# GpSimd makes every fourth low half of the first mixer's weights, from the second dense product to the output projection

## The chip, the cores and the metric

One core of one Trainium2 chip runs the kernel. The metric is the device time of one execution in microseconds; the median of three executions stands for the kernel. The profile is of one further execution.

## The reference

Two blocks act on a sequence x of 256 rows and 1024 columns in fp32, one after the other. The change lies in the first one's mixer:

```python
mod = silu(c) @ w_ada + b_ada
sh1, sc1, g1, sh2, sc2, g2 = split(mod, 6)
h = rms_norm(x) * (1 + sc1) + sh1
proj = h @ w_in                        # 1024 x 3592
q_a, k_a, v_a, qk_m, v_m, o_m, gates = split(proj)
attn = head_rms_norm(moba_attention(rope(q_a), rope(k_a), v_a))
q_m, k_m = split(silu(causal_conv(qk_m)))
hm = head_rms_norm(mlstm(q_m, k_m, v_m, gates)) * sigmoid(o_m)
x = x + g1 * (concat(attn, hm) @ w_out)   # 1024 x 1024
x = x + g2 * hier_moe(rms_norm(x) * (1 + sc2) + sh2)   # 4 groups x 8 experts
```

The second block has a differential attention, a grouped-query attention with axial ropes, and two feed-forward parts.

## The kernel before

**Weights.** All weights are cut into units of 128 x 4096 fp32 (2 MB), which SyncE loads in a fixed order (`prefetch`, L304) into a ring of five slots; a slot is free again when the last reader of its unit is done. In the expert part that follows the first mixer the ring has four slots more, and SyncE is asked ahead to fill all nine.

**Split products.** An fp32 product is made of three products in the format fp32r. `split` (L511) takes a piece of 128 x 512 of a unit `w`: ScalarE rounds it to the high half `wh` (L518), VectorE subtracts it to get the low half `wl` (L520), and `mm3` (L523) issues three matmuls on TensorE: high by high (L525), then one with each low half (L526, L527). In `dense` the `wl` product is L527, in `dense_t` and `rows_into` the products run with weights as the fixed or the moving operand, so `wl` is read by L526 or L527. In the first mixer `wh` and `wl` have four buffers each, so ScalarE can make a high half only when TensorE is done with the one four before it. `behind` (L505) can tie a low half to stand behind a named instruction; it counts down and is used for a few of them.

**The first mixer.** `w_in` is multiplied unit by unit: q (before the change's place), k, v, then the gates and the mLSTM's parts; then the attention and the mLSTM, woven with those products (`weave`, L1100, the generators `mixers` and `dense_work`), and the output projection with `w_out`. Beside the products, `mixed` (L820) and `beside` interleave the products of the adaLN modulation: `ada_cols` on VectorE (L456, a product of 128 x 1024 with its sum, 32 in all) and `ada` on TensorE (L433). The rope sums of q and k are on GpSimd (L700, L703), fed by products on VectorE that read PSUM (L698 to L702); TensorE turns the result (L795). GpSimd's queue also issues the loads of small constants (`load`, L872), and scales `sub_g` (L955). In the mLSTM part VectorE makes the conv products (L1010), ScalarE its silu (L1013), VectorE the score products (L1069).

**Order.** A tile scheduler puts every engine's instructions into one order from the program and from estimated times; each engine then runs its own list in that order and waits on semaphores for what the others make. So moving instructions from one engine to another can change the order of others too. The names in the rows below are the scheduler's: `wl_1337` is one certain low half, `wh_1336` its high half, `w_868` the unit it is cut from.

Of the kernel before, what the change touches and what calls it, by code (L numbers as in the profile page):

```python
# [10 lines left out]
F32 = mybir.dt.float32  # L11
# [174 lines left out]
def block_pair_kernel(ctx: ExitStack, tc: tile.TileContext, d, out):  # L186
    nc = tc.nc
    ve, se, po, te, sy = nc.vector, nc.scalar, nc.gpsimd, nc.tensor, nc.sync
    cnt = [0]

    def mk(pool, shape, dt, tag, **kw):
        cnt[0] += 1
        return pool.tile(shape, dt, tag=tag, name=f"{tag}_{cnt[0]}", **kw)
# [29 lines left out]
    def psum_g():  # L223
        return mk(pp, [128, 512], F32, "g")
# [82 lines left out]
    def take(name):  # L307
        prefetch(pos[0] + sum(n for _, n in slots["pools"]))
        got, w = loaded[pos[0]]
        assert got == name, (got, name)  # L310
        loaded[pos[0]] = None
        pos[0] += 1
        return w
# [73 lines left out]
    def weave(*flows):  # L387

        live = [[0, n, steps] for steps, n in flows]
        while live:  # L390
            f = min(live, key=lambda f: (f[0] + 0.5) / f[1])
            f[0] += 1
            if next(f[2], live) is live:
                live.remove(f)

    def attention(n, ready, score, value, norm, turn, turn_ready=lambda: True):


        held, late = [], []

        def values():
            p, i, e = held.pop(0)
            value(p, i, e)
            if i == n - 1:
                late.append((p, norm(p)))

        for p in range(4):
            while not ready(p):
                yield
            for i in range(n):  # L410
                held.append((p, i, score(p, i)))
                if len(held) > 1:
                    values()
                if late and i >= n // 2 and turn_ready():
                    turn(*late.pop(0))
                yield
        while held:
            values()
            yield
        while not turn_ready():  # L420
            yield
        while late:
            turn(*late.pop(0))
# [49 lines left out]
    def beside(steps, vfill, nv, fill, n_p):  # L473

        done = 0
        for i, _ in enumerate(steps):
            while (done + 1) * 8 <= (i + 1) * 4 * nv:
                next(vfill)
                done += 1
            yield  # L480
        for _ in range(n_p):
            next(fill, None)
            yield
# [11 lines left out]
    def spread(m, *gs):  # L495

        for j in range(4):
            ps = psum_g()
            te.matmul(ps, ident[:, 32 * j:32 * j + 1].to_broadcast([128, 128]), m, start=True, stop=True)
            se.copy(gs[j // 2][:, j % 2 * 512:(j % 2 + 1) * 512], ps)  # L500

    parts = [None, 5]

    chain = [None, 0]
    nth_chain = itertools.count()  # L505

    def behind():

        if chain[1] == 0:
            return nullcontext()  # L510
        chain[1] -= 1  # L511
        return tc.issue_after(chain[0])

    def split(w):

        wh = mk(parts[0], [128, 512], F32R, "wh", bufs=parts[1])
        wl = mk(parts[0], [128, 512], F32R, "wl", bufs=parts[1])
        se.copy(wh, w)  # L518
        with behind():
            ve.tensor_sub(wl, w, wh.bitcast(F32))  # L520
        return wh, wl

    def mm3(ps, ah, al, bh, bl, first, last):  # L523
# [9 lines left out]
    def dense(w, hi, lo, evict):  # L533

        pss = [psum_g() for _ in range(TT)]
        for k in range(DC):
            wh, wl = split(w[:, k * 512:(k + 1) * 512])
            for t in range(TT):
                s = slice(t * 128, (t + 1) * 128)
                mm3(pss[t], hi[k][:, s], lo[k][:, s], wh, wl, k == 0, k == DC - 1)  # L540
            yield
        for t in range(TT):
            evict(t, pss[t])

    def dense_t(w, hi, lo, evict, bank):

        pss = [bank(), bank()]
        for k in range(DC):
            wh, wl = split(w[:, k * 512:(k + 1) * 512])
            for c in range(4):  # L550
                o = pss[c // 2][:, (c % 2) * T:(c % 2 + 1) * T]
                cs_ = slice(c * 128, (c + 1) * 128)
                mm3(o, wh[:, cs_], wl[:, cs_], hi[k], lo[k], k == 0 and c % 2 == 0, k == DC - 1 and c % 2 == 1)
            yield
        for i in range(2):
            evict(i, pss[i])
# [56 lines left out]
    def turn_into(hi, lo, gain, done, nh, k0=0):  # L613

        def f(p, oc):
            ps = psum()[:, :nh * T].rearrange("p (h n) -> p h n", h=nh)
            for t in range(TT):
                for h in range(nh):
                    te.transpose(ps[:, h, t * 128:(t + 1) * 128], oc[:, t, h, :], ident)
            for h in range(nh):  # L620
                scale_into(hi, lo, gain)(k0 + nh * p + h, ps[:, h, :])
            done.extend(range(k0 + nh * p, k0 + nh * (p + 1)))
        return f

    def out_proj(name, hi, lo, acc, done):

        late = []
        for u in range(2):
            w = take(name)
            for k in range(4 * u, 4 * u + 4):  # L630
                while not k in done:
                    yield
                yield from rows_into(w[:, k % 4 * D:(k % 4 + 1) * D], [k], hi, lo, acc, 0, 7, 3 * (k > 5), late)
# [186 lines left out]
    def mixed(n, steps):  # L820
        return beside(steps, vfill, MIXV[n], fill, MIXP[n])
# [49 lines left out]
    def load(v, src):  # L871
        tc.keep_in_program_order(po.dma_start(v, src))  # L872
        return v
# [4 lines left out]
    qk_g = load(mk(base, [128, 256], F32, "qk_g"), bcast(d["qk_g"], 0, 256)).rearrange("p (a n) -> p a n", a=2)  # L878
    grid = load(mk(base, [128, 256], F32, "grid"), d["const_x"][:, X_CX:X_N])

    for _ in mixed(0, range(8)):
        pass
    for n, ev in ((0, None), (1, ev_qk(kT, store_k)), (2, lambda t, ps: se.copy(va[:, t, :], ps))):
# [117 lines left out]
    def conv_work(n):  # L1001
        def ev(i, ps):
            for a in range(2):
                c = 4 * n + 2 * i + a
                u = ps[:, a * T:(a + 1) * T]
                acc = qkm[:, c, :]
                se.activation(acc, u, AF.Identity, bias=conv[:, c, 4:5], scale=conv[:, c, 3:4])
                for j in range(3):
                    z = 3 - j
                    ve.scalar_tensor_tensor(acc[:, z:], u[:, :T - z], conv[:, c, j:j + 1], acc[:, z:],  # L1010
                                            op0=OP.mult, op1=OP.add)
            if n == 1 and i == 1:
                se.activation(qkm, qkm, AF.Silu)  # L1013

        yield from dense_t(take("w_in"), hi, lo, ev, psum_g)
# [8 lines left out]
    def router_work():  # L1024

        ps = psum_g()
        for k in range(DC):
            te.matmul(ps[0:36, 0:1], wr[:, k, :], fill_col[:, k:k + 1], start=k == 0, stop=k == DC - 1)
        ve.tensor_mul(wr, wr, fill_col[:, 8:16, None].to_broadcast([128, DC, 36]))
        lT = t1([36, 128])  # L1030
        ve.tensor_add(lT, ps[0:36, 0:1].to_broadcast([36, 128]), bcol.to_broadcast([36, 128]))
        te.transpose(ps[:, 128:164], lT, ident[0:36, 0:36])
        se.copy(br, ps[:, 128:164])

    def dense_work():
        for n in range(2):
            yield from mixed(3 + n, conv_work(n))
        yield from mixed(5, dense(take("w_in"), hi, lo,
                                  lambda t, ps: se.copy(vx[:, t, :, 0:128], ps.rearrange("p (h e) -> p h e", h=4))))
        stage["vx"] = True  # L1040
        sig = mk(paa, [128, TT, 512], F32, "va")
        yield from mixed(6, dense(take("w_in"), hi, lo, lambda t, ps: se.activation(sig[:, t, :], ps, AF.Sigmoid)))
        so.append(sig)
        yield from fill
        g.extend((mk(pa, [128, D], F32, "g1"), mk(base, [128, D], F32, "g2")))
        spread(gm, *g)
        router_work()
        acc.extend([psum_g(), psum_g()] for _ in range(TT))
        yield from out_proj("w_out", oh, ol, acc, done)
# [43 lines left out]
    def mixers():  # L1093
        yield from attention(2, lambda p: True, score, value, norm,
                             turn_into(oh, ol, lambda k: og[:, k:k + 1], done, 1))
        while not stage["vx"]:
            yield
        yield from attention(2, lambda h: True, mscore, mvalue, mnorm, mturn, lambda: len(so) > 0)

    weave((mixers(), WEAVE[2][0]), (dense_work(), WEAVE[2][1]))  # L1100
    g1, g2 = g
    attn_a.close()
    ring2, ring2_close = new_pool("ring2", "right")
# [563 lines left out]
```

## Time and profile before

| what | value |
|---|---|
| median of 3 executions | 1333.07 us (1332.79 to 1334.86) |
| profiled execution | 1335.57 us |
| its span | 1333.5 us (2.07 us lie around it) |
| busy in the span: TensorE, VectorE, ScalarE, GpSimd | 1122.0 (84%), 659.8 (49%), 487.8 (37%), 145.4 (11%) us |
| GpSimd instructions counted | 194 |
| mean rate of the DMA engines | 298 GB/s |

The span is measured from the first to the last instruction on the core. The first mixer ends at about 204 us, the expert part begins there, and from 233 to 640 us it is the expert products and their weights. A busy share over the whole span says little about any one of these stretches, so the rows below are of stretches.

### The profile page before, as it was taken

The numbers are of one execution on the slowest core, as the hardware profiler recorded it, in microseconds if no ns is written. First come the engines' busy times: TensorE is split into PE (matmuls) and PEld (weight loads), VectorE is DVE, ScalarE is ACT, GpSimd is POOL, SyncE is SP. The second block draws the span as 40 slices with busy tenths as digits, with TensorE's granted clock in tenths as the row PEclk, the third lists the DMA queues.
The fourth block names the chain that finished last, engine by engine and source line by source line (L and its number), as shares of the span: only waits on it lengthen the run. The fifth ranks groups of instructions, "written<-read, shape, count | busy, mean of one in ns | idle before, by whom it ended". The sixth has DMA issues, their size and how long they took to land.

```text
span 1333.5 us, 19535 instructions
## 1 busy us (share of the span) xinstructions
PE 1122.0 (84%) x7627; PEld 814.5 (61%) x7627; DVE 659.8 (49%) x1564; ACT 487.8 (37%) x1061; POOL 145.4 (11%) x194
## 2 busy tenths in 40 slices
PE   6889997865656576666689999999999989999995
PEld 4667775431313132321267777998996766998994
DVE  4688885210202020211277777555556866555555
ACT  2445652000000000000146565554554564554552
POOL 1310000000000000000030002210114201210112
PEclk8998998988979787878889999999999999999998
DMA  9856997999999999989988746745448516745400
GB/s 385 352 215 255 392 376 326 428 425 429 426 427 427 427 426 428 417 363 427 427 333 320 294 189 268 287 181 193 164 162 330 219 47 244 306 174 192 182 25 31
DMA packets 29705, 397.37 MB, mean 298 GB/s; under 512 B 4172, under 2 KB 4572, under 8 KB 5544
## 3 DMA queue, kind: packets, MB, share of 16 engines
q1 hardware_dynamic: 28856, 395.22, 72.5%
q8 instruction: 61, 1.00, 0.3%
q0 software_dynamic: 464, 0.83, 0.2%
q14 instruction: 36, 0.29, 0.1%
q10 hardware_dynamic: 288, 0.02, 0.0%
HBM read 395.01 MB, written 1.05 MB: 297 GB/s over the span
## 4 chain that ended last, share of the span: by engine, by line
PE 40%; DMA 6%; DVE 4%; issue 2%; POOL 2%; ACT 1%; DVEq 0%; SPq 0%; ACTq 0%; POOLq 0%
PE b L526 6%; PE b L527 6%; PE b L525 6%; DMA w<-in_w_dram 6%; PE g L527 5%; PE g L525 5%; PE g L526 5%; DVE wl L520 1%; PE b L1414 1%; POOL x L658 1%; PE g L433 1%; PE b L1524 1%; PE b L1544 1%; PE b L1442 1%; PE b L588 0%
## 5 line engine op out<-in xcount | busy, mean ns | idle before, releaser
L520 DVE TENSOR_TENSOR wl<-w,wh 128x512 fp32r<-128x512 f32 x440 | 309.8, 709 | 198.9 <-ACT wh L518 198.1
L518 ACT CAST wh<-w 128x512 fp32r<-128x512 f32 x440 | 270.2, 620 | 248.7 <-PE b L526 108.5
L1237 PE MATMUL g<-w,xg 128*32 128x512 f32 x1024 | 155.6, 740 | 99.6 <-DMA w<-in_w_dram 93.8
L526 PE MATMUL b<-lo,wh 128*128 128x256 f32 x704 | 199.4, 283 | 0.1
L525 PE MATMUL b<-hi,wh 128*128 128x256 f32 x704 | 199.5, 283 | 0.0
L527 PE MATMUL b<-hi,wl 128*128 128x256 f32 x704 | 199.3, 283 | 0.0
L1237 PEld LDWEIGHTS g<-w,xg 128*32 128x32 f32 x1024 | 32.5, 122 | 215.4 <-DMA w<-in_w_dram 116.8
L526 PEld LDWEIGHTS b<-lo,wh 128*128 128x128 f32 x704 | 135.2, 192 | 0.4 <-POOL lo L599 0.3
L525 PEld LDWEIGHTS b<-hi,wh 128*128 128x128 f32 x704 | 135.2, 192 | 0.1
L527 PEld LDWEIGHTS b<-hi,wl 128*128 128x128 f32 x704 | 135.2, 192 | 0.0
L1242 DVE TENSOR_TENSOR k<-g,k 128x512 f32<-128x512 f32 x8 | 5.5, 692 | 244.7 <-PE g L1237 244.7
L526 PE MATMUL g<-wl,hi 128*128 128x512 f32 x224 | 89.7, 400 | 3.6 <-DVE wl L520 3.5
L525 PE MATMUL g<-wh,hi 128*128 128x512 f32 x224 | 89.8, 410 | 3.0 <-ACT wh L518 3.0
L527 PE MATMUL g<-wh,lo 128*128 128x512 f32 x224 | 89.3, 399 | 0.1
L1254 PE MATMUL g<-w,k 128*32 128x256 f32 x1024 | 67.4, 400 | 16.6 <-DMA w<-in_w_dram 15.1
L1241 ACT ACTIVATE k<-g 128x512 f32<-128x512 f32 x8 | 4.8, 597 | 192.2 <-PE g L1237 192.2
L1624 POOL TENSOR_TENSOR fl<-k,fh 128x256 fp32r<-128x256 f32 x44 | 41.7, 949 | 272.8 <-ACT fh L1622 272.8
L525 PE MATMUL g<-wh,fh 128*128 128x512 f32 x176 | 68.5, 389 | 0.0
L526 PE MATMUL g<-wl,fh 128*128 128x512 f32 x176 | 68.5, 389 | 0.0
L527 PE MATMUL g<-wh,fl 128*128 128x512 f32 x176 | 68.5, 389 | 0.0
L1254 PEld LDWEIGHTS g<-w,k 128*32 128x32 f32 x1024 | 32.0, 114 | 46.4 <-DMA w<-in_w_dram 18.2
L1244 ACT COPY k<-b 128x512 f32<-128x512 f32 x8 | 4.7, 586 | 148.9 <-PE b L795 148.9
(385 smaller groups left out, 1760.6 us busy)
## 6 DMA issues: line engine op xcount, KB each, us to landing
w<-in_w_dram SPq DMA_DIRECT2D x96, 2048.0 KB, 39.1
w<-in_ada_dram SPq DMA_DIRECT2D x36, 2048.0 KB, 8.6
w<-in_fin_dram SPq DMA_DIRECT2D x22, 2048.0 KB, 8.7
w<-in_fout_dram SPq DMA_DIRECT2D x10, 2048.0 KB, 7.5
w<-in_w_in_dram SPq DMA_DIRECT2D x7, 2048.0 KB, 12.8
w<-in_aqkv_dram SPq DMA_DIRECT2D x6, 2048.0 KB, 39.2
w<-in_bqkv_dram SPq DMA_DIRECT2D x3, 2048.0 KB, 9.4
w<-in_w_out_dram SPq DMA_DIRECT2D x2, 2048.0 KB, 13.0
```

The source lines that it names most:

```text
L433: te.matmul(ps[32 * j:32 * j + 32, :], cs[:, i:i + 1].to_broadcast([128, 32]), w[:, a, j, :], start=k == 0, stop=k == DC - 1)
L518: se.copy(wh, w)
L520: ve.tensor_sub(wl, w, wh.bitcast(F32))
L525: te.matmul(ps, ah, bh, start=first, stop=False, skip_group_check=True)
L526: te.matmul(ps, ah, bl, start=False, stop=False, skip_group_check=True)
L527: te.matmul(ps, al, bh, start=False, stop=last, skip_group_check=True)
L658: (po if (t, c) in on_pool else ve).tensor_add(x[t][:, s], x[t][:, s], tmp)
L1237: te.matmul(ps[32 * j:32 * j + 32, :], xg[:, k, c0:c0 + CAP], up(nm, k, j), start=k == 0, stop=k == DC - 1)
L1254: te.matmul(ps[32 * j:32 * j + 32, :], hT[:, f, 32 * j:32 * j + 32], down(q, f, j), start=f == 0, stop=f == 3)
L1414: te.matmul(ps[:, a, :], qTs[p][:, h, t * 128:(t + 1) * 128], kTs[p % 3][:, 2 * h + a, :], start=True, stop=True)
L1442: te.matmul(outs[p][:, 2 * t + h, :], pT[:, k, :], vs[p // 2][:, k, v0:v0 + 128], start=k == 0, stop=k == 1)
L1624: po.tensor_sub(w, sg, h.bitcast(F32))
```

## The change

A counter runs over the calls of `split` while the list `shared` holds a number; every fourth call then subtracts on GpSimd and not on VectorE. It is set to 4 ahead of the second dense product (k) and to 0 behind the `weave` that ends with the output projection. There are 65 calls of `split` in between, so 16 low halves go to GpSimd: `wl_601`, `wl_641`, `wl_725`, `wl_767`, `wl_937`, `wl_1083`, `wl_1337`, `wl_1458`, `wl_1556`, `wl_1598`, `wl_1657`, `wl_1773`, `wl_1971`, and, in the output projection, `wl_2087`, `wl_2129`, `wl_2163`. For these `behind` is not asked.

```diff
+    shared = [0]
+    nth_split = itertools.count(1)
...
         se.copy(wh, w)
-        with behind():
-            ve.tensor_sub(wl, w, wh.bitcast(F32))
+        if shared[0] and next(nth_split) % shared[0] == 0:
+            po.tensor_sub(wl, w, wh.bitcast(F32))
+        else:
+            with behind():
+                ve.tensor_sub(wl, w, wh.bitcast(F32))
         return wh, wl
...
+    shared[0] = 4
     for _ in mixed(0, range(8)):
         pass
...
     weave((mixers(), WEAVE[2][0]), (dense_work(), WEAVE[2][1]))
+    shared[0] = 0
```

Line numbers of the changed kernel are 3 higher behind L504, 6 higher behind `split` (its subtraction on GpSimd is L523, the one on VectorE L526), 7 higher behind the new line ahead of `mixed(0, ...)`, and 8 higher behind the `weave`. SyncE's order is the same in both. GpSimd's list is the old one with the 16 put in; those of TensorE, ScalarE and VectorE are rewritten between about 95 and 200 us.

GpSimd, from the first ropes of q (`k_174`, `k_180`) to those of k (`k_211`). Before:

```order
L700 TENSOR_TENSOR k_174_509<-k_175_510,k_176_511 128x8x32
L703 TENSOR_TENSOR k_174_509<-k_177_512,k_178_513 128x8x32
L700 TENSOR_TENSOR k_180_526<-k_181_527,k_182_528 128x8x32
L703 TENSOR_TENSOR k_180_526<-k_183_529,k_184_530 128x8x32
L872 DMA con_x_543<-in_const_x_dram 128x32
L872 DMA sub_g_545<-in_sub_g_dram 128x1
L872 DMA lam_547<-in_lam_dram 64x4
L872 DMA qk_g_549<-in_qk_g_dram 128x256
L872 DMA grid_551<-in_const_x_dram 128x256
L955 TENSOR_SCALAR sub_g_545<-sub_g_545 128x1
L700 TENSOR_TENSOR k_211_650<-k_212_651,k_213_652 128x8x32
```

With the change:

```order
L523 TENSOR_TENSOR wl_601<-w_257,wh_600 128x512
L706 TENSOR_TENSOR k_174_509<-k_175_510,k_176_511 128x8x32
L709 TENSOR_TENSOR k_174_509<-k_177_512,k_178_513 128x8x32
L706 TENSOR_TENSOR k_180_526<-k_181_527,k_182_528 128x8x32
L709 TENSOR_TENSOR k_180_526<-k_183_529,k_184_530 128x8x32
L878 DMA con_x_543<-in_const_x_dram 128x32
L878 DMA sub_g_545<-in_sub_g_dram 128x1
L878 DMA lam_547<-in_lam_dram 64x4
L878 DMA qk_g_549<-in_qk_g_dram 128x256
L878 DMA grid_551<-in_const_x_dram 128x256
L962 TENSOR_SCALAR sub_g_545<-sub_g_545 128x1
L523 TENSOR_TENSOR wl_641<-w_257,wh_640 128x512
```

`wl_601` stands ahead of the ropes of q, and `wl_641` behind the scaling of `sub_g`; the next row there is `wl_725`, ahead of the ropes of k.

VectorE about the unit `w_868` (a part of the mLSTM's input), `s_1123` being a factor of the softmax just before it (`s_1123` was made three rows above the first one shown). Before:

```order
L1010 SCALAR_TENSOR_TENSOR qkm_865<-g_871,conv_140,qkm_865 128x254
L341 TENSOR_SCALAR s_1132<-s_1130 128x4
L456 SCALAR_TENSOR_TENSOR w_888,part_710<-w_888,g_82_189 128x1024
L344 TENSOR_TENSOR s_1134<-s_1123,s_1132 128x4
L1010 SCALAR_TENSOR_TENSOR qkm_865<-g_871,conv_140,qkm_865 128x255
L347 SCALAR_TENSOR_TENSOR s_1136<-s_1134,s_1132 128x4
L520 TENSOR_TENSOR wl_1337<-w_868,wh_1336 128x512
L348 SCALAR_TENSOR_TENSOR s_1137<-s_1136,s_1132 128x4
L351 SCALAR_TENSOR_TENSOR s_1140<-s_1136,s_1134 128x4
L456 SCALAR_TENSOR_TENSOR w_888,part_710<-w_888,g_82_189 128x1024
L347 SCALAR_TENSOR_TENSOR s_1142<-s_1140,s_1137 128x4
L520 TENSOR_TENSOR wl_1354<-w_868,wh_1353 128x512
```

With the change:

```order
L675 TENSOR_REDUCE s_1127<-k_330_1125 128x4
L975 TENSOR_REDUCE s_1099<-b_1170 128x2
L682 SCALAR_TENSOR_TENSOR s_1123<-s_1127,s_1122 128x4
L1017 SCALAR_TENSOR_TENSOR qkm_865<-g_871,conv_140,qkm_865 128x255
L339 TENSOR_SCALAR s_1130<-s_1123 128x4
L456 SCALAR_TENSOR_TENSOR w_888,part_710<-w_888,g_82_189 128x1024
L341 TENSOR_SCALAR s_1132<-s_1130 128x4
L456 SCALAR_TENSOR_TENSOR w_888,part_710<-w_888,g_82_189 128x1024
L344 TENSOR_TENSOR s_1134<-s_1123,s_1132 128x4
L526 TENSOR_TENSOR wl_1354<-w_868,wh_1353 128x512
L347 SCALAR_TENSOR_TENSOR s_1136<-s_1134,s_1132 128x4
L456 SCALAR_TENSOR_TENSOR w_888,part_710<-w_888,g_82_189 128x1024
```

`wl_1337` is gone to GpSimd, `wl_1354` stands two L456 behind `s_1123` (three before), and the small steps L348 and L351 come behind it.

VectorE about the unit `w_1508`, in the mLSTM. Before:

```order
L520 TENSOR_TENSOR wl_1679<-w_1508,wh_1678 128x512
L1069 SCALAR_TENSOR_TENSOR pr_1642<-b_1638,pr_1642 128x128
L520 TENSOR_TENSOR wl_1738<-w_1508,wh_1737 128x512
L520 TENSOR_TENSOR wl_1751<-w_1508,wh_1750 128x512
L456 SCALAR_TENSOR_TENSOR w_1518,part_1431<-w_1518,g_83_190 128x1024 x3
L1069 SCALAR_TENSOR_TENSOR pr_1672<-b_1667,pr_1672 128x256
L456 SCALAR_TENSOR_TENSOR w_1518,part_1431<-w_1518,g_83_190 128x1024
L1069 SCALAR_TENSOR_TENSOR pr_1693<-b_1689,pr_1693 128x128
```

With the change:

```order
L526 TENSOR_TENSOR wl_1738<-w_1508,wh_1737 128x512
L456 SCALAR_TENSOR_TENSOR w_1518,part_1431<-w_1518,g_83_190 128x1024
L1076 SCALAR_TENSOR_TENSOR pr_1642<-b_1638,pr_1642 128x128
L456 SCALAR_TENSOR_TENSOR w_1518,part_1431<-w_1518,g_83_190 128x1024 x2
L1076 SCALAR_TENSOR_TENSOR pr_1672<-b_1667,pr_1672 128x256
L456 SCALAR_TENSOR_TENSOR w_1518,part_1431<-w_1518,g_83_190 128x1024
L1076 SCALAR_TENSOR_TENSOR pr_1693<-b_1689,pr_1693 128x128
L1089 TENSOR_TENSOR s_1700<-s_1699,gcol_843 128x2
L526 TENSOR_TENSOR wl_1751<-w_1508,wh_1750 128x512
```

`wl_1751` stood directly behind `wl_1738`; now four L456 and three score products (L1076, which were L1069) come in between. `wl_1773`, two rows further before, is GpSimd's.

## Rows read from the trace of the kernel before

**Rows 1.** The windows: busy time of each engine in four stretches of the first mixer (a stretch in us from the span's start and its length; then busy us and instruction count of TensorE, its weight loads, VectorE, ScalarE and GpSimd; granted TensorE clock as a share of 2.4 GHz; mean share of the 16 DMA engines; GB/s).

```profile
62.00:97.00 35.00, 29.10 (x172) 24.36 (x172) 31.75 (x68) 16.55 (x29) 7.68 (x15) 0.97 0.62 241
97.00:135.00 38.00, 34.75 (x243) 29.88 (x241) 31.79 (x91) 18.25 (x55) 0.00 (x0) 0.89 0.60 233
135.00:180.00 45.00, 43.83 (x254) 30.75 (x252) 41.76 (x134) 28.90 (x55) 0.00 (x0) 1.00 0.96 396
180.00:204.00 24.00, 24.00 (x112) 19.22 (x111) 20.53 (x63) 12.12 (x27) 1.32 (x2) 1.00 0.91 378
```

**Rows 2.** The list of waits from 62 to 205 us: engine and what it waited to do, what released it; us in total, number, longest.

```profile
ACT wh L518 <- PE g L527: 16.5, 19, 3.0
...
PE g L527 <- DVE wl L520: 7.0, 3, 3.2
```

**Rows 3.** The page's costliest groups, the low halves over the whole program: operation, shapes, count; busy us and mean ns; idle time before them and what ended most of it.

```profile
L520 DVE TENSOR_TENSOR wl<-w,wh 128x512 fp32r<-128x512 f32 x440 | 309.8, 709 | 198.9 <-ACT wh L518 198.1
```

**Rows 4.** The windows again (columns as in rows 1), of the router with the expert dispatch and of the expert stretch.

```profile
217.00:233.00 16.00, 15.57 (x126) 8.58 (x130) 5.35 (x23) 4.66 (x11) 0.00 (x0) 0.87 0.54 215
233.00:640.00 407.00, 266.77 (x2196) 109.80 (x2188) 61.50 (x148) 23.01 (x49) 1.84 (x2) 0.86 1.00 421
```

**Rows 5.** The timeline of VectorE and GpSimd at two places late in the program, where both work at once: start us, duration us, engine, line, operation, shapes, count (idle time before it, and what ended that).

```profile
816.40 1.28 POOL L658 TENSOR_TENSOR x<-x,wl 128x512 f32<-128x512 f32 x1 [27.93 <-DVE wl L657]
...
818.48 1.66 POOL L658 TENSOR_TENSOR x<-x,wl 128x512 f32<-128x512 f32 x1 [0.80 <-DVE wl L657]
...
819.64 1.05 DVE L658 TENSOR_TENSOR x<-x,wl 128x512 f32<-128x512 f32 x1
...
853.67 0.94 POOL L1624 TENSOR_TENSOR fl<-k,fh 128x256 fp32r<-128x256 f32 x1 [8.15 <-ACT fh L1622]
...
853.92 0.42 DVE L1620 TENSOR_TENSOR k<-b,k 128x256 f32<-128x256 f32 x1
```

**Rows 6.** The timelines of ScalarE (one row, `wh_600`) and GpSimd from 48 to 72 us (columns as in rows 5): the first ropes of q, the scaling of `sub_g`, the first and the last rope sum of k.

```profile
48.95 0.62 ACT L518 CAST wh<-w 128x512 fp32r<-128x512 f32 x1 [0.76 <-PE g L527]
...
49.80 0.75 POOL L700 TENSOR_TENSOR k<-k,k 128x256 f32<-128x256 f32 x1 [3.17 <-DVE k L699]
...
61.13 0.24 POOL L955 TENSOR_SCALAR sub_g<-sub_g 128x1 f32<-128x1 f32 x1 [5.16 <-DMA sub_g<-in_sub_g_dram]
65.44 0.74 POOL L700 TENSOR_TENSOR k<-k,k 128x256 f32<-128x256 f32 x1 [4.07 <-DVE k L699]
...
71.24 0.72 POOL L703 TENSOR_TENSOR k<-k,k 128x256 f32<-128x256 f32 x1
```

**Rows 7.** The timeline of TensorE from 50 to 73 us: the transposes behind the ropes (L795) and the product that waits for `wl_641` (L526).

```profile
51.30 0.66 PE L795 MATMUL b<-con,k 128*128 128x128 f32 x4 [0.35 <-POOL k L703]
...
62.33 0.51 PE L526 MATMUL g<-wl,hi 128*128 128x512 f32 x1 [1.93 <-DVE wl L520]
...
72.02 0.66 PE L795 MATMUL b<-con,k 128*128 128x128 f32 x4 [1.04 <-POOL k L703]
```

**Rows 8.** The timeline of VectorE at that place: `wl_641` is the first of these two low halves.

```profile
61.60 1.28 DVE L520 TENSOR_TENSOR wl<-w,wh 128x512 fp32r<-128x512 f32 x2
```

**Rows 9.** The timelines of VectorE and TensorE about 100 us: `wl_1083`, and the first product that reads it.

```profile
99.07 0.68 DVE L520 TENSOR_TENSOR wl<-w,wh 128x512 fp32r<-128x512 f32 x1
...
101.05 0.39 PE L527 MATMUL g<-hi,wl 128*128 128x256 f32 x1
```

**Rows 10.** The timelines of VectorE and TensorE from 117 to 123 us: an L456, `wl_1337` (119.10), `wl_1354` (121.07), and the first product that reads each.

```profile
117.42 1.22 DVE L456 SCALAR_TENSOR_TENSOR w<-w,g 128x1024 f32<-128x1024 f32 x1
...
119.10 0.68 DVE L520 TENSOR_TENSOR wl<-w,wh 128x512 fp32r<-128x512 f32 x1
...
121.07 0.68 DVE L520 TENSOR_TENSOR wl<-w,wh 128x512 fp32r<-128x512 f32 x1
...
119.84 0.58 PE L527 MATMUL g<-hi,wl 128*128 128x256 f32 x1 [3.17 <-DVE wl L520]
...
122.14 0.41 PE L527 MATMUL g<-hi,wl 128*128 128x256 f32 x1
```

**Rows 11.** The windows, of the stretch behind that wait.

```profile
120.00:124.00 4.00, 4.00 (x19) 4.00 (x20) 4.00 (x13) 0.62 (x1) 0.00 (x0) 0.50 0.00 0
```

**Rows 12.** The timelines of VectorE and ScalarE about 145 us: one conv product, the activation-table load and the silu.

```profile
143.66 0.48 DVE L1010 SCALAR_TENSOR_TENSOR qkm<-g,conv,qkm 128x255 f32<-128x255 f32 x1
...
144.54 1.28 ACT L1013 ACT_TABLE_LOAD   x1
145.84 1.92 ACT L1013 ACTIVATE qkm<-qkm 128x2048 f32<-128x2048 f32 x1
```

**Rows 13.** The timelines of VectorE and TensorE from 157 to 163 us: `wl_1738` and `wl_1751` (one row for the two), the first two L456 behind them, and the first product that reads `wl_1751`.

```profile
157.69 1.29 DVE L520 TENSOR_TENSOR wl<-w,wh 128x512 fp32r<-128x512 f32 x2 [0.22 <-ACT wh L518]
158.90 1.22 DVE L456 SCALAR_TENSOR_TENSOR w<-w,g 128x1024 f32<-128x1024 f32 x1
...
160.04 1.22 DVE L456 SCALAR_TENSOR_TENSOR w<-w,g 128x1024 f32<-128x1024 f32 x1
...
162.83 0.39 PE L526 MATMUL g<-wl,hi 128*128 128x512 f32 x1
```

**Rows 14.** The timelines of VectorE and TensorE at the end of the output projection: one of its last low halves, and the first product that reads it.

```profile
197.90 0.69 DVE L520 TENSOR_TENSOR wl<-w,wh 128x512 fp32r<-128x512 f32 x1 [0.58 <-ACT wh L518]
...
200.08 0.40 PE L526 MATMUL g<-wl,ohi 128*128 128x512 f32 x1
```

## The prediction, made before the changed kernel ran

> **What bounds the kernel now.** I read the windows first, because a share over the whole span mixes stages. From 62 us to the end of the first mixer at about 204 us TensorE is busy 29.10 of 35, 34.75 of 38, 43.83 of 45 and 24.00 of 24 us, and VectorE 31.75, 31.79, 41.76 and 20.53 us in the same stretches [rows 1]. So TensorE is the bound from 135 us on, and before that the two engines are close, with some 9 us in which TensorE stands. GpSimd is nearly empty (7.68, 0, 0 and 1.32 us). The list of waits says who waits for whom: TensorE lost 7.0 us in three waits for a low half `wl` (made on VectorE, L520), the longest 3.2, while ScalarE's `wh` waited 16.5 us for TensorE to give buffers back [rows 2]. One low half costs VectorE 0.709 us on average [rows 3]; it can start 0.6 after the one before it.
>
> What a shift in the mixer is worth: in the router the transfers are at 0.54, and from 233 to 640 us at 1.00 of what 16 DMA engines take [rows 4]. The ring is full when the mixer ends, and the expert weights go on only when expert products free slots. So a mixer that ends later by d makes the expert stretch start and end later by d, and nothing behind it gives d back. I count d one to one.
>
> **Prices.** The moved operation has no row of before: GpSimd with two SBUF inputs of 128x512. The nearest is the gated sum L658 on GpSimd, of that shape: 1.28 us, and 1.66 where VectorE also works on two SBUF tensors; VectorE's own sum beside it then took 1.05 instead of the 0.68 of [rows 3] [rows 5]. So a moved half costs GpSimd 1.28 to 1.66, on VectorE it saves 0.61, and it may cost VectorE up to 0.6 (the part of 1.28 that a blocked sum waits). But the sum L1620, which reads one operand from PSUM, took 0.42 while GpSimd was inside a 0.94 us operation [rows 5]. It depends on what VectorE has in hand: column products L456 and low halves, with two SBUF tensors, would be blocked; ropes, reduces and conv products, fed from PSUM, would not. I take a block for half of the 16 moves.
> The Trainium skill, "SBUF — State Buffer", section "Who interferes with whom", states this as an exclusive lock: a VectorE instruction with two SBUF inputs and a GpSimd instruction that reads SBUF never run together, and one with at most one SBUF input is free; the two rows agree. Taken for every move, this is the third rival below.
>
> **The change, stretch by stretch.** 16 low halves leave VectorE, 16 x 0.61 = 9.8 us of its issue time, for GpSimd, 16 x 1.28 = 20.5 us. SyncE's order of loads is the same; TensorE's, ScalarE's and VectorE's orders are rewritten between about 95 and 200 us. A low half matters only where TensorE takes it at once, so I walked those.
>
> a) 48 to 73 us. `wl_601` now stands on GpSimd ahead of the four rope sums of k_174 and k_180. Its `wh`, begun at 48.95 [rows 6], is there at 49.6, so it ends at 50.9, and the ropes, which began at 49.80 [rows 6], begin 1.1 later; TensorE's L795 at 51.30, which had already waited for them [rows 7], goes with them; that much TensorE gets back in its next stop, if nothing else moves. The constant loads on GpSimd's queue come later by the same. Behind them stands the scaling of `sub_g` (L955), which waited 5.16 us for its load and ran at 61.13 [rows 6], and `wl_641` is now behind that. Before, `wl_641` ended at about 62.28 and TensorE, which had stood 1.93 us, went on at 62.33 [rows 7, 8]. Now: 61.13 + 1.1 + 0.24 + 1.28 = 63.75, so +1.5. If the load lands when it did, it is 62.65 (+0.4); with the 1.66 price and a blocked VectorE, +2.3. `wl_725` stands ahead of the ropes of k_211 and k_217, whose last sum at 71.24 releases TensorE at 72.02 after 1.04 of idle [rows 6, 7]; GpSimd had stood 4.07 us before those ropes at 65.44 [rows 6], and `wl_725` waits for a buffer that TensorE frees after its restart, so both move with that restart and it is counted once. I take **+1.5** (0.4 to 2.3).
>
> b) 98 to 105 us. `wl_1083` sat on VectorE at 99.07 and TensorE used it at 101.05 [rows 9]; on an idle GpSimd it is ready some 10 us earlier, and TensorE's order now takes its products ahead of the column products and the L987 block. I take **-0.5**, between 0 and -1.2 (the VectorE time around it).
>
> c) 115 to 123 us: the largest prize. TensorE stands 3.17 us until `wl_1337` at 119.84, and then runs at a granted clock of 0.50 (1.2 GHz) in 120 to 124 [rows 10, 11]. GpSimd is idle here, so `wl_1337` comes early and this wait goes. What is late next is `wl_1354`, which started at 121.07 and was taken by TensorE at 122.14 [rows 10]: in VectorE's new order two L456 (they start 1.14 apart, [rows 13]) still stand between the softmax factor and it, and one ahead of that factor. Without `wl_1337` (0.6), three of the small steps that now follow it (0.08 each) and up to 0.7 of idle time that the early L456 fills, it ends between 120.2 and 120.9, so 1.2 to 1.9 before that use. But TensorE then stands 2 to 3 us one half later, so the clock falls as before; and half of the gain is lost where `wl_1337` and `wl_1458` on GpSimd meet L456 and low halves on VectorE. I take **-0.8** (0 to -1.9; if the wait shrank under 1 us, -3.2 and more).
>
> d) 135 to 151 us. ScalarE's table load and the silu of `qkm` (1.28 and 1.92 us, at 144.54 and 145.84 [rows 12]) now stand ahead of `wh_1555`, and three more conv products L1010 (0.48, [rows 12]) ahead of `wl_1533`, a low half that TensorE takes as soon as it is ready. 3 x 0.40 = 1.2 later on VectorE, less the one or two low halves taken out before it: **+0.5** (-0.5 to +1.5).
>
> e) 157 to 170 us. Before, `wl_1751` ran directly behind `wl_1738` (the pair from 157.69 [rows 13]), 3.85 us before TensorE used it at 162.83. Now four L456, 1.14 apart, and three L1069 (0.25 to 0.34) stand between: 158.3 + 4 x 1.15 + 0.9 = 163.8, and its end 164.4. TensorE would wait 1.6, less what the two low halves taken away (`wl_1657`, `wl_1773`, 1.2) bring VectorE forward. I take **+0.5** (0 to +2.5).
>
> f) Output projection. Its low halves ended 1.5 us and more before their use (`wl` at 197.90, TensorE at 200.08 [rows 14]); GpSimd takes 0.6 longer for one, or 1.0 in a block. 0, and if that slack were gone, 0.5 at most for each of three.
>
> Sum: 1.5 - 0.5 - 0.8 + 0.5 + 0.5 = **+1.2 us**. The profiled execution took 1335.57 (span 1333.5 and 2.07 around it); the change there would be at 1336.8. That execution is 2.5 above the median of 1333.07, so I add the sum to the median: **1334.3**.
>
> **Rivals.** *The relief pays.* If VectorE is the real bound from 62 to 135 us and GpSimd's operations fall beside PSUM-fed work, TensorE's wait at 116 goes (3.2), and with it part of the slow clock behind it, and b gives 1.2: -4.6 or so, 1328.5. For it: VectorE busy 4.00 of 4.00 us in 120 to 124 [rows 11], GpSimd at 0 from 97 to 180. Against it: `wl_1354` stands behind the same L456, and TensorE is at 43.83 of 45 from 135 on, where nothing can be won. Deciding point: whether TensorE still stands over 2 us near 117. Chance 0.22.
>
> *The new order costs (slower).* The low half `wl_1751` behind four L456: it decides if VectorE reaches `wl_1738` no earlier than the 157.7 of before. Then TensorE waits at 162.8 for 1.6, and 2.5 with the L456 blocked by `wl_1773` on GpSimd, and with a at its upper end (2.3), b and c at 0: +4.8, 1337.9. For it: the order itself, and TensorE has no other idle time there to hide it. Against it: VectorE has two low halves less in this unit. Chance 0.24.
>
> *The lock counts everywhere.* Each moved half blocks VectorE for 1.28 - 0.69 = 0.59, so nothing is relieved and VectorE's line grows: 16 x 0.59 = 9.4, 1342.5. Against it: more than half of the places have reduces, ropes or conv products in hand, and half of the moved ones have slack. Chance 0.06. It is the rule of that page of the Trainium skill, taken literally.
>
> **How the numbers follow.** 0.2% of 1333 is 2.7 us, about what can be told from no change. My own case, 0.48: between 1330.5 and 1336.5 by the bounds of a to e that can come together; it lies mostly within 0.2%, with some on the slow side. Faster: 0.22. Slower: 0.24 + 0.06 + 0.03 of my case = 0.33. Same: 0.45. The range reaches from the first rival's 1328.0 to 1339.0, over the second; out of it are the third and the far end of the first.
>
> **What would show it.** Right: in the profile after, TensorE's stop at 62.3 ends at 63 to 64 and is released by GpSimd; the stop at 116 to 119 is shorter but there, released by VectorE, with the clock at 0.5 behind it; a new stop near 163; 16 GpSimd subtractions of 1.28 to 1.7 us; VectorE's busy time down by about 10 us less what the blocks add; the DMA rate going up to 1.00 near 225 us [rows 4] later by 1 to 2 us. Wrong: that point earlier by over 2.5 us, or a TensorE stop of over 3 us that none of a to e names, or L456 and low halves as short as before beside GpSimd's work.

## The result, and the profile after

The changed kernel takes 1350.1 us (median of 4 executions, 1347.03 to 1352.23) against 1333.96 (1332.79 to 1335.93) for the kernel before in the same comparison: ratio 1.0109, 95% interval 1.0085 to 1.0133, so about 14.5 us slower (the two medians differ by 16.1, the two profiled executions by 13.5). One execution in the experiments below, of the run that moves `wl_1083` alone, took 2743 us and is left out of its ratio. The prediction said 1334.3, between 1328.0 and 1339.0: too low by 16, and outside its range. The profiled execution took 1349.08, its span is 1347.1.

Most of the loss is there when the first mixer ends. The first row normalisation of the router (ScalarE) starts at 204.80 us in the trace before and at 217.10 in the trace after, 12.3 later; the spans differ by 13.6. At the kernel's start, ahead of the first moved half, the two traces already differ by 0.8 (TensorE's L768 at 33.72 stands at 34.51), which the change cannot explain.

The page after, its line of busy times and two groups (columns as in rows 3):

```profile
PE 1132.1 (84%) x7627; PEld 817.0 (61%) x7627; DVE 660.3 (49%) x1548; ACT 488.6 (36%) x1061; POOL 172.3 (13%) x210
...
L526 DVE TENSOR_TENSOR wl<-w,wh 128x512 fp32r<-128x512 f32 x424 | 301.2, 714 | 205.3 <-ACT wh L521 204.5
```

This is the line to read first. VectorE has 16 low halves less (424 against 440), which at 0.68 is 10.9 us. Its busy time went from 659.8 to 660.3. Nothing was relieved: about as much came back as longer instructions, 9.9 us when measured against the write-only run below, which has the same order of VectorE at 650.4.

The list of groups on GpSimd, with the moved halves in it (line, shapes and count; busy us, mean ns; idle before, released by ScalarE's `wh`):

```profile
L523 POOL TENSOR_TENSOR wl<-w,wh 128x512 fp32r<-128x512 f32 x16 | 25.4, 1588 | 120.2 <-ACT wh L521 120.2
```

The windows of after in the stretches of [rows 1]:

```profile
62.00:97.00 35.00, 26.73 (x153) 22.28 (x151) 26.44 (x48) 15.99 (x24) 15.09 (x18) 0.95 0.59 230
97.00:135.00 38.00, 32.73 (x215) 26.89 (x216) 31.86 (x92) 15.46 (x46) 4.72 (x4) 0.91 0.58 230
135.00:180.00 45.00, 41.08 (x232) 31.45 (x231) 37.88 (x100) 25.18 (x51) 7.09 (x4) 0.96 0.81 328
180.00:204.00 24.00, 24.00 (x134) 16.73 (x133) 22.02 (x82) 16.10 (x35) 3.79 (x3) 1.00 0.79 312
```

TensorE, VectorE and ScalarE are all less busy from 62 to 97 and from 135 to 180 us than before: they wait. (The same window holds somewhat earlier work than before, since the work has moved.) From 135 to 180 the DMA share fell from 0.96 to 0.81: in SyncE's timeline the loads of this stretch are issued 3.5 to 9.4 us later, those of `w_out` from 161.53 and not from 152.81.

TensorE's stops, from its timeline after; they answer to [rows 7, 10]:

```profile
53.18 0.66 PE L801 MATMUL b<-con,k 128*128 128x128 f32 x4 [1.43 <-POOL k L709]
...
64.09 0.50 PE L532 MATMUL g<-wl,hi 128*128 128x512 f32 x1 [1.79 <-POOL wl L523]
...
75.59 0.66 PE L801 MATMUL b<-con,k 128*128 128x128 f32 x4 [2.82 <-POOL k L709]
...
76.43 0.63 PE L533 MATMUL g<-wh,lo 128*128 128x512 f32 x1
...
116.85 0.38 PE L533 MATMUL g<-hi,wl 128*128 128x256 f32 x1 [2.16 <-DVE wl L526]
...
127.30 0.39 PE L533 MATMUL g<-hi,wl 128*128 128x256 f32 x1 [0.70 <-DVE wl L526]
...
130.43 0.39 PE L533 MATMUL g<-hi,wl 128*128 128x256 f32 x1 [1.43 <-DVE wl L526]
...
157.70 0.50 PE L532 MATMUL g<-wl,hi 128*128 128x512 f32 x1 [1.95 <-DVE wl L526]
...
207.00 0.41 PE L625 MATMUL b<-con,oc 128*128 128x128 f32 x2 [1.47 <-DVE oc L1097]
```

The stop at 64.09 is the predicted one, released by GpSimd. The one at 75.59 is new in size (72.02, after 1.04, before), and behind it products take 0.63 where they took 0.39: the granted clock fell to its lower level for some 3.4 us (0.53 in the window 76 to 79), another 1.6 lost.

GpSimd's timeline after, at five of the moved halves and the ropes of k, answers to [rows 6]:

```profile
50.45 1.31 POOL L523 TENSOR_TENSOR wl<-w,wh 128x512 fp32r<-128x512 f32 x1 [3.03 <-ACT wh L521]
...
61.06 2.97 POOL L523 TENSOR_TENSOR wl<-w,wh 128x512 fp32r<-128x512 f32 x1
66.30 1.32 POOL L523 TENSOR_TENSOR wl<-w,wh 128x512 fp32r<-128x512 f32 x1 [2.27 <-ACT wh L521]
67.58 1.19 POOL L706 TENSOR_TENSOR k<-k,k 128x256 f32<-128x256 f32 x1
68.73 1.70 POOL L709 TENSOR_TENSOR k<-k,k 128x256 f32<-128x256 f32 x1
...
74.81 0.72 POOL L709 TENSOR_TENSOR k<-k,k 128x256 f32<-128x256 f32 x1
...
113.88 1.30 POOL L523 TENSOR_TENSOR wl<-w,wh 128x512 fp32r<-128x512 f32 x1 [20.92 <-ACT wh L521]
...
154.72 2.31 POOL L523 TENSOR_TENSOR wl<-w,wh 128x512 fp32r<-128x512 f32 x1 [2.04 <-ACT wh L521]
```

And VectorE's timeline after, at the same times and at more of them:

```profile
62.84 1.74 DVE L526 TENSOR_TENSOR wl<-w,wh 128x512 fp32r<-128x512 f32 x1
...
113.91 0.48 DVE L1017 SCALAR_TENSOR_TENSOR qkm<-g,conv,qkm 128x254 f32<-128x254 f32 x1
114.31 0.89 DVE L348 SCALAR_TENSOR_TENSOR s<-s,s 128x4 f32<-128x4 f32 x1
115.12 0.15 DVE L351 SCALAR_TENSOR_TENSOR s<-s,s 128x4 f32<-128x4 f32 x1
...
128.38 1.24 DVE L348 SCALAR_TENSOR_TENSOR s<-s,s 128x4 f32<-128x4 f32 x1
...
155.84 1.22 DVE L339 TENSOR_SCALAR s<-s 128x4 int32<-128x4 int32 x1
156.97 0.68 DVE L526 TENSOR_TENSOR wl<-w,wh 128x512 fp32r<-128x512 f32 x1
...
195.31 1.28 DVE L348 SCALAR_TENSOR_TENSOR s<-s,s 128x2 f32<-128x2 f32 x1
...
203.12 1.03 DVE L347 SCALAR_TENSOR_TENSOR s<-s,s 128x2 f32<-128x2 f32 x1
```

Read the two together. The half on GpSimd at 61.06 waits inside its own 2.97 us until 62.84, while VectorE goes through a low half and an L456, and then VectorE's low half at 62.84 waits for it: 1.74 instead of 0.68. At 154.72 GpSimd waits for an L456, and when that ends at 155.84 GpSimd goes first: L339, a step on four numbers of each row, takes 1.22 instead of 0.16, and the low half behind it at 156.97 is the one that TensorE's stop at 157.70 waits for. Paired in this way, ten of the 16 halves have an instruction of VectorE beside them that is longer than its like, by 0.56 to 1.13 us, 9.1 us in all; six of the ten are steps on two or four numbers of a row. So a block costs on average 0.91 us, more than the 0.68 that the half cost VectorE before, be the blocked step large or tiny. Of the six halves that blocked nothing, four fell where VectorE stood idle (those at 75.49, 84.31, 91.68 and 210.30).

### The profile page after: what moved, and what is told of

Same layout as the page of the kernel before. It is cut to its first block, busy times and chain, and to the rows that moved or that the text cites. A ratio compares the mean times of both kernels' runs of the same rounds, so it can differ in the third digit from the quotient of the medians.

```text
span 1347.1 us, 19543 instructions
## 1 busy us (share of the span) xinstructions
PE 1132.1 (84%) x7627; PEld 817.0 (61%) x7627; DVE 660.3 (49%) x1548; ACT 488.6 (36%) x1061; POOL 172.3 (13%) x210
## 4 chain that ended last, share of the span: by engine, by line
PE 42%; DMA 5%; DVE 4%; issue 2%; POOL 2%; ACT 1%; DVEq 0%; ACTq 0%; POOLq 0%; SPq 0%
PE b L532 6%; PE b L533 6%; PE b L531 6%; PE g L531 5%; PE g L533 5%; PE g L532 5%; DMA w<-in_w_dram 5%; PE g L433 1%; PE b L1422 1%; DVE wl L526 1%; POOL x L664 1%; PE b L1532 1%; PE g L1262 1%; PE b L1552 1%; PE g L594 1%
## 5 line engine op out<-in xcount | busy, mean ns | idle before, releaser
L526 DVE TENSOR_TENSOR wl<-w,wh 128x512 fp32r<-128x512 f32 x424 | 301.2, 714 | 205.3 <-ACT wh L521 204.5
L1245 PE MATMUL g<-w,xg 128*32 128x512 f32 x1024 | 158.8, 754 | 98.6 <-DMA w<-in_w_dram 92.4
L1262 PEld LDWEIGHTS g<-w,k 128*32 128x32 f32 x1024 | 32.3, 116 | 45.1 <-DMA w<-in_w_dram 14.5
L456 DVE SCALAR_TENSOR_TENSOR w<-w,g 128x1024 f32<-128x1024 f32 x48 | 59.6, 1244 | 0.1
## 6 DMA issues: line engine op xcount, KB each, us to landing
w<-in_w_in_dram SPq DMA_DIRECT2D x7, 2048.0 KB, 12.3
w<-in_w_out_dram SPq DMA_DIRECT2D x2, 2048.0 KB, 11.1
```

The lines of the kernel that those rows point to most:

```text
L456: ve.scalar_tensor_tensor(w[:, s], w[:, s], 1.0, cond, op0=OP.mult, op1=OP.mult, accum_out=part[:, 4 * u + j:4 * u + j + 1])
L1245: te.matmul(ps[32 * j:32 * j + 32, :], xg[:, k, c0:c0 + CAP], up(nm, k, j), start=k == 0, stop=k == DC - 1)
L1262: te.matmul(ps[32 * j:32 * j + 32, :], hT[:, f, 32 * j:32 * j + 32], down(q, f, j), start=f == 0, stop=f == 3)
```

## The experiments

Every run was timed in five rounds beside the kernel before on the same chip; the ratio is to that kernel's time there, with a 95% interval. Theory Q is the queue on GpSimd, L the block between the two engines (lock), O the rewritten order, N the lateness of a half made on GpSimd. Where nothing else is said, only the condition in `split` differs from the change (`nth` counts the calls of `split` while `shared` is set):

```diff
-        if shared[0] and next(nth_split) % shared[0] == 0:
+        nth = next(nth_split) if shared[0] else 1
+        if nth % 4 == 0 and nth <= 12:
             po.tensor_sub(wl, w, wh.bitcast(F32))
```

**Which halves cost: the early three** (the condition above).

> Only wl_601, wl_641 and wl_725 go to GpSimd; TensorE's and ScalarE's orders are those of the kernel before. Theory Q (queue: the three halves push the rope sums on GpSimd, and through them TensorE, later: 1.1 at 53 us and 3.4 at 75.6 us in the profile of the change): +4.5 us, 1338.5. Theory L (lock: each half costs what it blocks on VectorE, 0.6): +1.8. Theory O (order: the loss comes from the rewritten order between 95 and 200 us): 0.

Measured: 1.0027 (1.0014 to 1.0041), +3.6 us. Between L and Q, nearer to Q; the stops at the ropes are there with the order of before:

```profile
54.07 0.66 PE L802 MATMUL b<-con,k 128*128 128x128 f32 x4 [1.43 <-POOL k L710]
...
74.36 0.66 PE L802 MATMUL b<-con,k 128*128 128x128 f32 x4 [2.82 <-POOL k L710]
```

**The other thirteen**: `nth % 4 == 0 and nth > 12`.

> All 16 but those three go to GpSimd; TensorE's and ScalarE's orders are those of the change. Theory Q: the rest costs nothing, so about 0 (1334). L: 13 x 0.6 = +8 (1342). O: nearly all of the loss, +11 to +15 (1345 to 1349). Q and O together: +10 (1344).

Measured: 1.0064 (1.0046 to 1.0082), +8.5 us. Q alone falls: 8.5 of the loss of 14.5 us are behind the ropes. 8.5 fits L (8) and is below O (11 to 15), but with an interval from 6.1 to 11.0 us this run alone leaves O's lower end, and "Q and O together" (10), open.

**The three of the output projection**: `nth % 4 == 0 and nth > 52`.

> Only the three of the output projection (wl_2087, wl_2129, wl_2163) go to GpSimd. The prediction's term f: 0. L: up to 1.1 at each small operation of VectorE that is blocked, and the profile of the change has a stop of 1.47 us at 207 us behind such a chain: +1 to +2. O: 0.

Measured: 1.0003 (0.9991 to 1.0015). No cost is seen, as term f had it, though the interval (-1.2 to 2.0 us) still holds L's +1 to +2. Two steps of VectorE were blocked in this run's trace, L347 at 182.81 (1.24 us) and at 189.53 (1.17), and TensorE has no stop behind them: the price of a block is paid only where VectorE is waited for.

**GpSimd writes only.**

```diff
-            po.tensor_sub(wl, w, wh.bitcast(F32))
+            po.memset(wl.bitcast(F32), 0.0)
+            po.memset(wl.bitcast(F32), 0.0)
```

> The 16 halves are not subtracted: GpSimd fills their tiles with zeros, twice over each (write only, about 0.53 each, 1.06 in all), in the same places and with VectorE's and ScalarE's orders those of the change. L: GpSimd reads nothing, so VectorE is not blocked and its 11 us of relief show: busy time of VectorE near 649 us, and the time 1334 to 1340 (a part of Q remains). O: unchanged, 1345 to 1350. Q alone: 1346 to 1349, since 1.06 stands where 1.31 stood.

Measured: 0.9988 (0.9975 to 1.0001). With VectorE's and ScalarE's orders those of the change, and TensorE's but for three of its 7627 matmuls, the whole loss is gone, and VectorE's relief shows for the first time, 9.4 us of its busy time:

```profile
PE 1125.2 (84%) x7627; PEld 812.7 (61%) x7627; DVE 650.4 (49%) x1548; ACT 488.2 (37%) x1061; POOL 162.5 (12%) x226
```

O falls. TensorE's stops here are, in the list of its matmuls, the very ones that stand at 116.85, 127.30, 130.43 and 157.70 in the change:

```profile
109.92 0.39 PE L535 MATMUL g<-hi,wl 128*128 128x256 f32 x1 [1.42 <-DVE wl L528]
...
118.86 0.39 PE L535 MATMUL g<-hi,wl 128*128 128x256 f32 x1 [0.70 <-DVE wl L528]
...
120.91 0.39 PE L535 MATMUL g<-hi,wl 128*128 128x256 f32 x1 [0.36 <-DVE wl L528]
...
146.45 0.50 PE L534 MATMUL g<-wl,hi 128*128 128x512 f32 x1 [0.75 <-DVE wl L528]
```

In the change they are longer by 0.74, 0, 1.07 and 1.20. The steps blocked shortly ahead of the first, third and fourth (L348 at 114.31 and at 128.38, L339 at 155.84) had lost 0.74, 1.09 and 1.06, and the second has none ahead of it. So where TensorE waits for VectorE, a block on a tiny step reaches it about whole.

And the relief is worth next to nothing: 9.4 us less on VectorE gave 1.6 us, with an interval that reaches to no gain. One thing was left unsettled: these fills wait for no `wh`.

**The same, behind `wh`.**

```diff
-            po.tensor_sub(wl, w, wh.bitcast(F32))
+            po.tensor_copy(wl[:, 0:8], wh[:, 0:8])
+            po.memset(wl[:, 8:512].bitcast(F32), 0.0)
+            po.memset(wl[:, 8:512].bitcast(F32), 0.0)
```

> As the write-only run, but GpSimd first copies 8 columns of the high half, so its fills wait for ScalarE's wh as the subtraction does; the low halves are not subtracted (zeros). Orders of VectorE, ScalarE those of the change. Theory L (GpSimd's reads block VectorE and are blocked by it): within 3 us of the kernel before, VectorE's busy time near 650. Theory N (not the block, but that the moved half is ready only about 1.3 after its wh, and stands in GpSimd's queue): +10 to +15.

Measured: 1.0010 (0.9995 to 1.0025), busy time of VectorE 651.0. The run did only half of what was expected of it: copy and fills write different columns, and GpSimd's timeline shows the fills behind the copy for eight of the 16 halves, both ahead of it for seven and one on either side for one. The eight, `wl_725`, `wl_767`, `wl_1083`, `wl_1337`, `wl_1458`, `wl_1598`, `wl_1657` and `wl_1773`, are about as late as in the change and read almost nothing, and the whole run costs 1.3 us, not 10 to 15. So N falls for these eight; the next run, in which all 16 wait for `wh`, bears on the others. What this one does cost is at the ropes, TensorE's stop there being 1.68 against 1.04 before and 2.82 in the change:

```profile
74.98 0.66 PE L804 MATMUL b<-con,k 128*128 128x128 f32 x4 [1.68 <-POOL k L712]
```

**One operand read.**

```diff
-            po.tensor_sub(wl, w, wh.bitcast(F32))
+            po.tensor_copy(wl, wh.bitcast(F32))
```

> GpSimd makes each of the 16 by a copy of the high half (one operand read in place of two; the low half's value is left out). L, if one operand is enough to block: +8 to +15 and VectorE's busy time at 655 to 661. L, if only two operands block: within 3 us of before and 649 to 651. N: as long as the copy takes, +8 to +14, and VectorE's busy time at 650.

Measured: 1.0011 (0.9996 to 1.0026), VectorE's busy time 654.3: just under the range of L's first case, while the time is that of its second. The copy takes 0.61 free, half of the subtraction, and it blocks and is blocked too, for its own length. GpSimd and VectorE about 124 us:

```profile
122.70 1.68 POOL L524 CAST wl<-wh 128x512 fp32r<-128x512 f32 x1 [9.17 <-ACT wh L521]
...
123.83 0.56 DVE L348 SCALAR_TENSOR_TENSOR s<-s,s 128x4 f32<-128x4 f32 x1
```

GpSimd waits for the L456 that began at 122.69, and the step L348 (0.15 alone) then waits for GpSimd. So one operand read by GpSimd is enough for a block; at some 3.3 us more on VectorE than with fills the time does not show it. N falls here too: all 16 come behind their `wh`, if only by 0.6 us, and of its +8 to +14 us 1.5 are measured.

**Four pieces.**

```diff
-            po.tensor_sub(wl, w, wh.bitcast(F32))
+            for i in range(0, 512, 128):
+                po.tensor_sub(wl[:, i:i + 128], w[:, i:i + 128], wh[:, i:i + 128].bitcast(F32))
```

> GpSimd subtracts each of the 16 in four pieces of 128 columns (about 0.4 each, 1.7 in all). L, with the block held for one instruction: a small operation of VectorE waits 0.4 at most and not 1.1, and so does a piece of GpSimd for VectorE; the loss falls to +4 to +9, VectorE's busy time to 652 to 657. N: a half is ready 0.4 later than in the change: +14 to +18.

Measured: 1.0071 (1.0046 to 1.0097), +9.5 us, VectorE's busy time 656.3. The sign is L's, though the time ends half a us over L's band: GpSimd is busy longer (181.7 against 172.3), yet the estimate lies under that of the change (1.0109; the two intervals just overlap). A small step waits for a piece, not for a half:

```profile
123.51 0.41 DVE L348 SCALAR_TENSOR_TENSOR s<-s,s 128x4 f32<-128x4 f32 x1
```

**Twice over.**

```diff
             po.tensor_sub(wl, w, wh.bitcast(F32))
+            po.tensor_sub(wl, w, wh.bitcast(F32))
```

> GpSimd subtracts each of the 16 twice over (2.6 us). L: blocks come twice, +22 to +32, VectorE's busy time 668 to 674. N: each moved half is ready 1.3 later; the three early ones and those that TensorE waits for lose it, +18 to +24, VectorE's busy time 660.

Measured: 1.0193 (1.0173 to 1.0213), +25.8 us, and

```profile
PE 1134.5 (83%) x7627; PEld 819.3 (60%) x7627; DVE 671.4 (49%) x1548; ACT 488.6 (36%) x1061; POOL 192.6 (14%) x226
```

16 more subtractions on GpSimd, none on VectorE, and VectorE is busy 11.1 us more than in the change; the time rises by 0.84% of 1335, 11.2 us. The time alone would not decide, since N's upper end (24) lies in its interval (23.1 to 28.5); VectorE's busy time does, 671.4 as L had it and not 660.

**Three halves beside which VectorE was not blocked**: `nth in (16, 20, 44)`.

> Only wl_767, wl_937 and wl_1657 go to GpSimd: in the profile of the change no instruction of VectorE was longer beside them. TensorE's and ScalarE's orders are those of the kernel before. Theory L: no block, so no loss, 0 to -1.5 us, VectorE's busy time 657.5 to 658. A fixed price per half that GpSimd makes (late by 0.6 and more): +1 to +3, as the three early ones cost 3.6.

Measured: 1.0005 (0.9992 to 1.0017). No loss is seen; but the run is not the test that was planned. In this kernel two of the three did block VectorE, `wl_767` an L456 and `wl_1657`, at 153.28, a low half (1.38 at 153.74), and VectorE's busy time (659.5) shows no relief. What it shows is two more blocks without a price; a fixed price of up to 2.3 us for the three stays within the interval. GpSimd and VectorE at the first:

```profile
71.37 1.79 POOL L524 TENSOR_TENSOR wl<-w,wh 128x512 fp32r<-128x512 f32 x1
...
71.92 2.33 DVE L456 SCALAR_TENSOR_TENSOR w<-w,g 128x1024 f32<-128x1024 f32 x1
```

**The order, by one half that rewrites it**: `nth == 24`, `wl_1083`.

> Only wl_1083 goes to GpSimd; beside it too VectorE was not blocked in the profile of the change. This one move rewrites TensorE's order in 335 rows (100 to 165 us). L: within 1 us of before. O, the order costs time by itself: +3 to +8.

Measured: 0.9996 (0.9982 to 1.0011). O falls once more, for this part of the order.

**The largest wait of before**: `nth == 28`, `wl_1337`.

> Only wl_1337 goes to GpSimd, the half whose wait of 3.17 us at 119.84 is the largest of the kernel before; TensorE's order changes in 304 rows. The relief rival: -3 to -5 us. The prediction's term c: the wait passes to wl_1354, -0.8 (0 to -1.9). L: one block of 0.7 on a chain of small operations, 0 to +1. O: +3 and more.

Measured: 1.0001 (0.9989 to 1.0014). The relief rival falls. The half is ready at 108 us instead of 119.8, and TensorE stands as long as before, one half later, for `wl_1354`:

```profile
119.68 0.58 PE L534 MATMUL g<-hi,wl 128*128 128x256 f32 x1 [3.76 <-DVE wl L527]
```

The runs in the order of VectorE's busy time, where the 16 places and VectorE's order are the change's throughout:

| what GpSimd does at the 16 places | VectorE busy, us | ratio to before |
|---|---|---|
| writes only | 650.4 | 0.9988 |
| writes only, behind `wh` | 651.0 | 1.0010 |
| copies `wh` | 654.3 | 1.0011 |
| subtracts in four pieces | 656.3 | 1.0071 |
| subtracts (the change) | 660.3 | 1.0109 |
| subtracts twice | 671.4 | 1.0193 |

## Why the prediction was wrong

**The step that failed** stands in the prices: "I take a block for half of the 16 moves", with a price of "up to 0.6". It was wrong in three ways. The share was too low: ten of the 16, and not eight, blocked a step of VectorE. The price was too low: such a step lost 0.91 on average and up to 1.13, so 9.1 us in all where half of the moves at 0.6 make 4.8. What I overlooked is what VectorE has in hand after the step beside which GpSimd starts. The conv product at 113.91 ran its 0.48 freely beside the subtraction at 113.88, as forecast, but 1.3 us outlast such a step, and the next was L348, which lost 0.74. I had priced only large instructions; a step of 0.15 that waits 1.1 is as bad. And the share that I did take never reached the sum as a whole: a block stood in a, c and e as part of a range.

The third rival had the mechanism, with a chance of 0.06 and 1342.5, and its 9.4 us on VectorE are close to the 9.1. Its time was too low by 8: it left out what blocks do on GpSimd (a mean of 1.59 us for a half, up to 2.97) and what TensorE's stops add through the clock. The rule of the Trainium skill, "SBUF — State Buffer", section "Who interferes with whom", an exclusive lock for the whole instruction, held for steps with two SBUF operands: L348 took 1.24 beside a subtraction, 0.41 beside pieces, 0.56 beside a copy, and was not seen blocked by fills. The same section frees a step with one SBUF input only "outside the 2-port perf modes", which the prediction's sentence on it leaves out, and counts `tensor_scalar` among those that can enter such a mode; L339, a `tensor_scalar` with one SBUF input, took 1.22 beside a subtraction.

**a) The ropes: mis-sized, and one term left out.** Forecast +1.5. The stop for `wl_641` ended at 64.09 (63.75 forecast), released by GpSimd, though for another reason than the one given: the scaling of `sub_g` ran at 60.84, no later than before, and the 1.7 came from the wait inside the 2.97 us. L795 at 51.30 moved to 53.18, 1.1 beside the 0.8 of the start. What failed is "both move with that restart and it is counted once". `wl_725` occupied GpSimd from 66.30 to 67.62, and the rope sums behind it met VectorE's L456 and low halves: 1.19 and 1.70 where 0.74 stood before. The chain of memsets, casts and the last rope sum is back to back on GpSimd, so all of that arrived at TensorE: 72.02 became 75.59, 3.57 later, and with the lower clock behind it the stretch ended some 4.3 later than the start's 0.8. The early three alone measured 3.6.

**b) and c) right in mechanism, undone by blocks.** `wl_1083` and `wl_1337` were ready early, and the wait passed on, as said; alone they gave 0.9996 and 1.0001. In the write-only run the stretch from the products of the gates (at 77.81 before) to the column products (L433, at 135.06 before) won 3.7 us, more than the 1.3 of b and c; in the change it lost 1.3. The stops at 116.85, 127.30 and 130.43 (2.16, 0.70, 1.43) are 4.3 in all against 3.2 before; without blocks they were 2.5. The wait for `wl_1354`, forecast at 2 to 3 us, is the one of 0.70 at 127.30; the largest, at 116.85, belongs to a half that stands later in VectorE's new order, which the prediction did not name. The forecast of a low clock behind the stop held in part: 0.64 in 116 to 120 us, but 1.00 from 124 to 132.

**d) mis-sized:** forecast +0.5, the largest loss of all. The column products begin 6.4 later than before (all but two of the 32), and the first product of the mLSTM (L1058, at 154.75 before) 11.3 later, so 4.9 of the loss lie here, with the stop at 157.70 behind L339, and a granted clock of 0.64 from 157 to 161, as their last part. In the write-only run, with VectorE's order the same, the two stand 3.1 and 1.6 earlier than before, so the stretch lost 1.5. So about a third of d goes with the order and two thirds with the blocks; that the order as a whole costs nothing is its gain in b and c, which the blocks took away.

**e) The place was wrong:** no stop near 163; from the first mLSTM product to 170 us of before nothing more was lost, so the second rival (the new order at `wl_1751`) did not come true.

**f) right alone** (1.0003), but in the change TensorE stops 1.47 at 207.00 behind the mLSTM's small steps, two of them blocked, at 195.31 and 203.12; the write-only run has no such stop.

The relief rival falls by the write-only run: even a relief that costs nothing is worth 0.12% with an interval from 0.25 to nothing. (The lower end of the range, 1328.0, is named as that rival's, whose own sum is 1328.5; nothing hangs on it.) That a shift of the mixer passes to the end held: 12.3 at the router, 13.6 at the end.

What stays open is how the 8.5 us of the thirteen late halves divide over single halves: those tried alone or in threes showed no cost, so the price seems to depend on several of them falling into one stretch where VectorE is never idle; no run shows that by itself.

## What to carry to other kernels

Before moving an elementwise operation from VectorE to GpSimd, list what VectorE runs during its whole length on GpSimd, the tiny steps too, and count a block wherever two operands come from SBUF, and, as L339 shows here, for a `tensor_scalar` that reads one. If the sum of blocks is as long as what leaves VectorE, nothing is relieved, and the moved result is later and stands in GpSimd's queue besides. The check in a profile is one number: VectorE's busy time must fall by about what was taken off it. And look for the next late result before paying for an early one: here the first wait was 3.2 us long, and removing its half moved it one half on.

## What was not expected of the hardware

A `tensor_scalar` on 128x4 int32 with one SBUF operand (L339) was blocked like the rest: 1.22 us beside GpSimd's subtraction and 0.57 beside its copy, where it takes 0.16 alone. And beside write-only fills, where no step with two SBUF operands was seen blocked, it took 0.60, and the next such step, L341, 0.50:

```profile
151.39 0.51 POOL L525 MEMSET wl<- 128x504 f32 x1
151.97 0.52 POOL L526 MEMSET wl<- 128x504 f32 x1
...
151.33 0.60 DVE L339 TENSOR_SCALAR s<-s 128x4 int32<-128x4 int32 x1
...
152.01 0.50 DVE L341 TENSOR_SCALAR s<-s 128x4 int32<-128x4 int32 x1
```

A GpSimd copy of 128x512 took 0.61 free and a fill 0.53, against 1.30 for the subtraction; and a copy of only 8 columns took 0.19 us free and 1.11 when it met an L456, so its length tells the block and not the work.
